# Tokens in their own order in x; the values of mixer A and of B's first group made token by token

## The chip, the cores and the metric

One Trainium2 chip, one of its cores. The metric is the time of one execution in microseconds of device time. The engines are named as in the profile: PE (matrix products; PEld is its loading of the stationary operand), DVE (vector), ACT (scalar), POOL, and SP, whose queue issues most DMAs.

## The reference, cut to what matters

x has 512 tokens of 1024 channels. One product makes queries, keys and values for two mixers, which read the same tokens:

```
proj = h @ w_in
qa, ka, va, qb, kb, vb = split(proj)                # rotation on the first 16 of every 64 channels of q and k
o_a = windowed attention, 16 query heads on 4 key heads, |i - j| <= 128, with a sink, blocks of 128 queries
o_b = for 4 head slots, three groups with (window, dilation) (128, 1), (512, 4), (2048, 16), merged by denominators
gates = sigmoid(h @ w_gate + b_gate)
mixed = g_a * (o_a @ w_br_a) + g_b * (o_b @ w_br_b)
h = layer_norm(a * h + mixed @ w_out)
h = layer_norm(a * h + (silu(h @ w_ff_gate) * (h @ w_ff_up)) @ w_ff_down)
```

Mixer A and the first group of B work on blocks of neighbouring tokens. The second and third groups of B take every 4th and every 16th token, so they work on residues: all tokens with the same remainder of their number by 4.

## The kernel before, in words

Every product is of 32-bit numbers, split in a rounded part (fp32r, "h") and the rest ("l"); one product of two such matrices takes three matrix instructions (h by h, h by l, l by h). A unit is 128 output channels by all 512 tokens: 8 slices of 128 input channels, 24 instructions of 512 columns. Its weights come as two tiles of 256 KB ("ws"), and each tile is split by a copy that rounds (line 333 on ACT or 335 on DVE) and a subtraction on DVE (354) into two slots of the class "whl"; there are 6 ws and 16 whl slots (65).

**x by residue.** The host lays out x so that the 512 columns are residue 0's 128 tokens, then residue 1's, and so on. The start (421 to 432) loads 8 tiles of x, and for each a copy writes the h part (429) and a DVE subtraction the l part (430, 431). With them, slice by slice, run three first units (939 to 942): keys ("k"), queries ("q") and values ("v") of mixer A, with weights cut in pieces of 128, 128 and 256 columns so that the first pieces come early (366 to 386, order by FIRST).

**Queries and keys.** A unit's result goes from PSUM to SBUF; its 32 rotated rows are sent by small DMAs on SP into a common tile (485), rotated by four DVE operations (496 to 502, a "turn", T in the order), and sent back (506). Then q_post (518), k_post (535) and k_sides (553) write the split parts. q_post and k_post bring the columns from residue order into blocks of 128 tokens for mixer A, by runs of 32 floats (510 to 516); k_sides serves the second and third groups, which need residue order, and reads straight on.

**Values** must have the tokens on the partitions. Mixer A's and those of B's first group are made as units, channels on the partitions, then copied (594 to 602) and turned on PE by 128x128 transposes (611), four for each pair of blocks; value_split (617) splits the turned block. The first group's blocks are shifted by 64 tokens. The values of the second and third groups are made directly (632 to 658): x's columns of one residue are the stationary operand, 512 channels of both groups the moving one, 96 instructions (650 to 652).

**Attention.** For mixer A (unit_a, 712) there are 16 blocks: scores (578, 579), a DVE operation that adds the mask (726), exp on ACT (730), a factor (666, 668), transposes of the probabilities (678), products with the values (743, 744), and an addition of two halves that writes the result by residue (754). Mixer B (unit_b, 773) does the same for three groups.

**The order** is not the code's. ORDER (74) names the steps; every operation gets a priority from the work on PE before it, and a scheduler (171) with modelled costs writes each engine's queue once, while the program is built. In ORDER, VA and V0 are the turned values, V the direct ones, q1 to q7 and Q../K.. units, A0 to A3 and B0 to B3 the attention, G and g gates (924), which fill PE; G sends its result to DRAM and it is fetched later. An engine does its queue in order.

Of the kernel before, what the change touches and what calls it, by code (L numbers as in the profile page):

```python
# [15 lines left out]
P = 128  # L16
# [45 lines left out]
FIRST = {("k", 0): (-1000, -998.2, -997.2), ("q", 0): (-998.8, -998.1, -997.1), ("v", 0): (-998.7, -998, -997),  # L62
         ("k", 1): (-996.9,), ("q", 1): (-996.7,), ("v", 1): (-996.6,),
# [11 lines left out]
VA q1 T G q2 A0 q3 q4 G k1 T G A1 q5 G q6 q7 T A2 G G A3 G  # L75
Q00 K00 T V Q02 K02 T V0 Q01 K01 T B0 B1 g Q10 K10 T g Q12 K12 T Q11 K11 T B2 B3 g7
# [212 lines left out]
def hybrid_layer(ctx: ExitStack, tc: tile.TileContext, wpack, xT, xtok, sink, bgate,  # L289
# [40 lines left out]

    def copy(eng, dst, src):
        if eng == ACT:
            nc.scalar.activation(dst, src, AF.Copy)  # L333
        else:
            nc.vector.tensor_copy(dst, src)
# [86 lines left out]
    for j in range(2):  # L422
        for w, u in (("k", U_KA), ("q", U_QA), ("v", U_VA)):
            first[w, j] = half_unit_by(u, j, ((0, S),) if j else CUTS, FIRST[w, j])
    for j in range(KD):
        st, ap = slot(F32, "xs"), FIRST["x"][j]
        load(st, xT[j], abs_prio=ap)
        th, tl = xtok_of(j)
        op(cp_alts(S), lambda e, j=j, st=st: copy(e, xh[j](), st.t), reads=[st], writes=[th], abs_prio=ap)
        op([(DVE, dve(S))], lambda e, j=j, st=st: nc.vector.tensor_tensor(  # L430
            xl[j](), st.t, f32(xh[j]()), op=ALU.subtract), reads=[st, th], writes=[tl], abs_prio=ap)
    cosT, sinT, mA, mB = slot(), slot(), slot(), slot()
    for t_, src, ap in ((cosT, ropec, -119.5), (sinT, ropes, -119.4)):
        for i in range(8):
            op([(POOL, 1.0)], lambda e, t_=t_, i=i, src=src: nc.gpsimd.dma_start(t_.t[16 * i:16 * i + 16], src[0:16]),
               writes=[(t_, i)], abs_prio=ap, moves=0.1)
    load(mA, maska, abs_prio=-119.3, dst=lambda: mA.t[:, :384])
# [36 lines left out]
    class Turn:  # L474
# [16 lines left out]
        def turn(self):  # L491
# [7 lines left out]
               reads=[*toks, *[(cosT, i) for i in range(8)]], writes=[t], prio=EV)  # L499
            op([(DVE, dve(S))], lambda e: nc.vector.tensor_tensor(w.t[r], w.t[r], sinT.t[r], op=ALU.mult),  # L500
               reads=[w, *[(sinT, i) for i in range(8)]], writes=[w], prio=EV)
# [8 lines left out]
    def view(ap, nt, src):  # L510

        if nt == 0:
            return ap
# [21 lines left out]
    def k_post(R, heads, nt):  # L535
# [15 lines left out]
    k_post.head = lambda h, hh, nt: h  # L551
# [32 lines left out]
    def turned_values(u, nt, turn_by=0, done=None):  # L584

        src = []
        w = S // nt
        for i in range(2):
            ps = done
            if i or not done:  # L590
                ps = bank("dense")
                feat_x(ps, unit(u + i))
            t = slot()

            def evac(e, t=t, ps=ps):
                s = view(ps.t, nt, True)
                if turn_by:
                    copy(e, view(t.t[:, turn_by * w:], nt - turn_by, False), s[:, :nt - turn_by])
                    copy(e, view(t.t[:, :turn_by * w], turn_by, False), s[:, nt - turn_by:])
                else:  # L600
                    copy(e, view(t.t, nt, False), s)

            op(cp_alts(S, True), evac, reads=[ps], writes=[t], prio=EV)
            src.append(t)
        res = []
        for b in range(NR):
            pb = bank("tb")

            def turn(e, pb=pb, b=b):
                for i in range(2):  # L610
                    nc.tensor.transpose(pb.t[:, i * P:(i + 1) * P], src[i].t[:, b * P:(b + 1) * P], ident.t)

            op([(PE, 0.22)], turn, reads=[*src, ident], writes=[pb])
            res.append(value_split(pb))
        return res

    def value_split(pb, c0=0):

        t = slot(F32R)
        v = lambda: t.t.rearrange("p (h c) -> p h c", h=4)  # L620
        s = lambda: pb.t[:, c0:c0 + 256].rearrange("p (h c) -> p h c", h=4)
        op(cp_alts(256, True), lambda e: copy(e, v()[:, :, 0:64], s()), reads=[pb],
           writes=[(t, "h"), (t, "room")], prio=EV)
        op([(DVE, dve(256))], lambda e: nc.vector.tensor_tensor(
            v()[:, :, 64:128], s(), f32(v()[:, :, 0:64]), op=ALU.subtract),
           reads=[pb, (t, "h")], writes=[(t, "l")], prio=EV)
        return t

    def vtok(t):
        return [(t, "h"), (t, "l")]  # L630

    def token_values():

        parts_ = []
        for k in range(KD):
            st, h, l = slot(F32, "ws"), slot(F32R, "whl"), slot(F32R, "whl")
            u, c = U_VB + k // 4, (k % 4) * 256
            load(st, wpack[u:u + 3:2, :, c:c + 256].rearrange("g p c -> p g c"),
                 dst=lambda st=st: st.t.rearrange("p (g c) -> p g c", g=2), prio=-LOOK)
            split(st, h, l, prio=-LOOK, hold=[(l, "room")])  # L640
            parts_.append((h, l))
        res = ([], [])
# [957 lines left out]
```

## Time and profile before

| | us |
|---|---|
| median of 3 runs (lowest to highest) | 781.55 (781.13 to 781.97) |
| the profiled execution, its time | 781.53 |
| the profiled execution, its span | 779.8 |
| PE busy in the span | 769.9 |
| DVE busy | 652.5 |
| ACT busy | 480.9 |
| POOL busy | 131.5 |

The span is from the first to the last instruction; the rest of the execution's time lies around it. Busy times of PE overlap from one matrix instruction to the next, so what PE does is read from the starts in the timeline. In a row of the timeline the numbers are start and duration in us, xN says how many instructions were merged, and brackets hold the idle time before it and who ended it. In a group's row stand the busy us, the mean ns of one, and the idle time before them. A window's row has the length, then busy us and count for PE, PEld, DVE, ACT and POOL, then the granted clock of PE (1.00 is full), the DMA share and GB/s.

### The profile page before, as it was taken

Reading aid. Unit: us, or ns where it says so; the run is one execution under the profiler, and the core shown is the slowest. Engines: PE = TensorE matmul, PEld = TensorE weight load, DVE = VectorE, ACT = ScalarE, POOL = GpSimd, SP = SyncE. Lnnn points to the kernel's source line nnn. Section 1 sums busy time; section 2 is a strip of 40 time slices with the busy share of each in tenths; the row PEclk is TensorE's granted clock in tenths of the full one; section 3 lists DMA queues with packets and bytes.
Section 4 is the critical chain, followed back from the end, with each engine's and each line's share of the span. In section 5 each row is a group of like instructions: output and inputs, shape, how many; then the busy total and the mean of one; then the engine's idle time right before and its main releaser. Section 6 shows DMA issues by size and latency. Waiting matters only on the chain.

```text
span 779.8 us, 13408 instructions
## 1 busy us (share of the span) xinstructions
PE 769.9 (99%) x4486; PEld 676.6 (87%) x4486; DVE 652.5 (84%) x1377; ACT 480.9 (62%) x1061; POOL 131.5 (17%) x304
## 2 busy tenths in 40 slices
PE   9999999999999999999999999999999999999996
PEld 5888888888888888888888899999999999999985
DVE  5689889898778999797687999887988889888697
ACT  5557787868757668794341667566655566555631
POOL 4100001100000801600011010242102331123002
PEclk9999999999999999999999999999999999999999
DMA  8642323213132324436373388689867987689102
GB/s 268 217 138 71 99 88 105 83 44 108 57 96 88 104 87 145 142 111 201 121 217 67 109 231 225 155 183 213 227 179 161 241 179 208 182 213 210 52 1 108
DMA packets 64901, 111.79 MB, mean 143 GB/s; under 512 B 8640, under 2 KB 12352, under 8 KB 64832
## 3 DMA queue, kind: packets, MB, share of 16 engines
q1 hardware_dynamic: 52656, 89.37, 35.5%
q0 software_dynamic: 12032, 21.50, 16.5%
q8 instruction: 35, 0.57, 0.3%
q14 instruction: 34, 0.28, 0.1%
q10 hardware_dynamic: 144, 0.07, 0.0%
HBM read 104.09 MB, written 3.93 MB: 139 GB/s over the span
## 4 chain that ended last, share of the span: by engine, by line
PE 93%; DVE 2%; ACT 1%; DMA 1%; issue 1%; SPq 1%; DVEq 0%
PE ps L457 11%; PE ps L456 11%; PE ps L458 11%; PE ps L1314 9%; PE ps L1313 9%; PE ps L1312 9%; PE ps L1441 4%; PE ps L1442 4%; PE ps L1443 4%; PE ps L1077 3%; PE ps L1079 3%; PE ps L1078 3%; PE ps L678 2%; PE ps L579 1%; PE ps L578 1%; PE ps L743 1%
## 5 line engine op out<-in xcount | busy, mean ns | idle before, releaser
L333 ACT ACTIVATE sl<-sl 128x512 fp32r<-128x512 f32 (+5 forms) x446 | 242.5, 571 | 65.9 <-DMA sl<-wpack 16.6
L1196 DVE TENSOR_TENSOR sl<-sl,sl 128x512 fp32r<-128x512 f32 (+3 forms) x304 | 169.9, 604 | 12.1 <-ACT sl L333 7.6
L333 ACT ACTIVATE sl<-ps 128x256 f32<-128x256 f32 (+4 forms) x206 | 88.6, 451 | 114.5 <-PE ps L1314 66.6
L456 PE MATMUL ps<-x,sl 128*128 128x512 f32 x336 | 133.7, 398 | 0.4 <-ACT sl L333 0.3
L457 PE MATMUL ps<-x,sl 128*128 128x512 f32 x336 | 131.9, 393 | 0.2 <-DVE x L430 0.2
L458 PE MATMUL ps<-x,sl 128*128 128x512 f32 x336 | 131.6, 392 | 0.0
L354 DVE TENSOR_TENSOR sl<-sl,sl 128x512 fp32r<-128x512 f32 x130 | 87.0, 687 | 9.3 <-ACT sl L333 6.5
L1266 POOL DMA_DIRECT2D sl<-wpack x44 | 39.8, 970 | 260.1 <-DMA sl<-wpack 111.6
L458 PEld LDWEIGHTS ps<-x,sl 128*128 128x128 f32 x336 | 63.1, 188 | 14.4 <-DVE sl L382 0.7
L1312 PE MATMUL ps<-x,sl 128*128 128x256 f32 x264 | 74.8, 283 | 0.0
L1314 PE MATMUL ps<-x,sl 128*128 128x256 f32 x264 | 74.7, 283 | 0.0
L1313 PE MATMUL ps<-x,sl 128*128 128x256 f32 x264 | 74.7, 283 | 0.0
L456 PEld LDWEIGHTS ps<-x,sl 128*128 128x128 f32 x336 | 63.2, 188 | 12.2 <-ACT x L333 1.0
L457 PEld LDWEIGHTS ps<-x,sl 128*128 128x128 f32 x336 | 63.3, 188 | 12.0 <-DVE x L430 1.8
L1196 DVE TENSOR_TENSOR sl<-sl,ps 128x512 f32<-128x512 f32 (+1 forms) x78 | 47.4, 611 | 25.7 <-PE ps L1314 16.6
L1312 PEld LDWEIGHTS ps<-x,sl 128*128 128x128 f32 x264 | 50.6, 192 | 0.5
L1313 PEld LDWEIGHTS ps<-x,sl 128*128 128x128 f32 x264 | 50.6, 192 | 0.5
L1314 PEld LDWEIGHTS ps<-x,sl 128*128 128x128 f32 x264 | 50.6, 192 | 0.0
L1314 PE MATMUL ps<-tw,sl 128*128 128x256 f32 x176 | 49.8, 283 | 0.0
L1313 PE MATMUL ps<-tw,sl 128*128 128x256 f32 x176 | 49.8, 283 | 0.0
L1314 PE MATMUL ps<-sl,sl 128*128 128x256 f32 x176 | 49.8, 283 | 0.0
L1313 PE MATMUL ps<-sl,sl 128*128 128x256 f32 x176 | 49.8, 283 | 0.0
(149 smaller groups left out, 1808.7 us busy)
## 6 DMA issues: line engine op xcount, KB each, us to landing
sl<-wpack SPq DMA_DIRECT2D x243, 256.0 KB, 3.4
sl<-wpack POOLq DMA_DIRECT2D x44, 256.0 KB, 5.2
wf<-wpack SPq DMA_DIRECT2D x36, 256.0 KB, 4.2
wf<-wpack POOLq DMA_DIRECT2D x36, 256.0 KB, 6.5
sl<-sl SPq DMA_DIRECT2D x88, 32.0 KB, 1.9
sl<-xT SPq DMA_DIRECT2D x8, 256.0 KB, 5.8
sl<-xtok SPq DMA_DIRECT2D x8, 256.0 KB, 2.7
gz<-sl SPq DMA_DIRECT2D x7, 256.0 KB, 2.2
```

The lines of the kernel that those rows point to most:

```text
L333: nc.scalar.activation(dst, src, AF.Copy)
L354: op([(DVE, dve(S))], lambda e: nc.vector.tensor_tensor(l.t, src.t, f32(h.t), op=ALU.subtract), reads=[src, h], writes=[l], prio=prio, abs ...
L456: mm(o, a, x0, start=(k == 0), stop=False)
L457: mm(o, a, x1, start=False, stop=False)
L458: mm(o, b, x0, start=False, stop=(k == nk - 1))
L1196: op([(DVE, dve(w))], lambda e: nc.vector.tensor_tensor(dst(), x(), y(), op=o), reads=reads, writes=writes, prio=prio)
L1266: return op([(POOL, 1.0)], lambda e: nc.gpsimd.dma_start(dst.t, wpack[u, :, j * S:(j + 1) * S], accum_op=ALU.add), reads=[dst], writes=[ds ...
L1312: mm(o, wh, bh[k](), start=(first and k == 0), stop=False, skip_group_check=True)
L1313: mm(o, wh, bl[k](), start=False, stop=False, skip_group_check=True)
L1314: mm(o, wl, bh[k](), start=False, stop=(k == 3), skip_group_check=True)
L1441: mm(ps.t, x0, w[0].t, start=(first and m == 0), stop=False, skip_group_check=True)
L1442: mm(ps.t, x0, w[1].t, start=False, stop=False, skip_group_check=True)
```

## The change

x is written token by token. The data come from DRAM by residue as before; the copies that split x, the rotation tables and the masks put them in order on the way, so that they write every fourth float (by_res and res_by are the two views). The values of A and of B's first group are made like those of the other groups, in one product of 512 columns (256 of A, 256 of B's first group) with 128 neighbouring tokens as the stationary operand, 96 instructions; turned_values and its 16 transposes go. The first group's shift by 64 tokens is made by splitting halves of 64 rows. In the direct values of the second and third groups the stationary operand is now every fourth column of x. Gates are written by residue from PSUM, and the views in q_post, k_sides and the addition of A now read every fourth float where they must go by residue; mixer A's queries and all k_post keys are read straight on.

In the start a second unit of queries ("r") takes the place of the first unit of values; the first tile of x is rounded on DVE alone.

```diff
-VA q1 T G q2 A0 q3 q4 G k1 T G A1 q5 G q6 q7 T A2 G G A3 G
-Q00 K00 T V Q02 K02 T V0 Q01 K01 T B0 B1 g Q10 K10 T g Q12 K12 T Q11 K11 T B2 B3 g7
+q2 VA T G A0 q3 q4 G k1 T A1 q5 G q6 q7 T A2 G G A3 G Q00 K00 T V Q02 K02 T Q01 K01 T B0 B1 g Q10 K10 T g Q12 K12 T Q11 K11 T B2 B3 g8
...
+    def by_res(ap):
+        return ap.rearrange("p (i r) -> p r i", r=4)
+    def res_by(ap):
+        return ap.rearrange("p (r i) -> p r i", r=4)
...
-        op(cp_alts(S), lambda e, j=j, st=st: copy(e, xh[j](), st.t), reads=[st], writes=[th], abs_prio=ap)
+        op(cp_alts(S)[1 if j == 0 else 0:], lambda e, j=j, st=st: copy(e, by_res(xh[j]()), res_by(st.t)), reads=[st], writes=[th], abs_prio=ap)
         op([(DVE, dve(S))], lambda e, j=j, st=st: nc.vector.tensor_tensor(
-            xl[j](), st.t, f32(xh[j]()), op=ALU.subtract), reads=[st, th], writes=[tl], abs_prio=ap)
+            by_res(xl[j]()), res_by(st.t), by_res(f32(xh[j]())), op=ALU.subtract), reads=[st, th], writes=[tl], abs_prio=ap)
...
+        op(cp_alts(S), lambda e, t_=t_, raw=raw: copy(e, by_res(t_.t), res_by(raw.t)), reads=[(raw, i) for i in range(8)],
+           writes=[t_], abs_prio=ap + 1)
...
-        if nt == 0:
+        if nt is None:
             return ap
-        if src:
-            return ap.rearrange("p (r t i) -> p t r i", r=4, t=nt)
-        return ap.rearrange("p (t r i) -> p t r i", r=4, t=nt)
+        if nt == 0:
+            return by_res(ap) if src else res_by(ap)
+        return ap.rearrange("p (t i r) -> p t r i" if src else "p (t r i) -> p t r i", r=4, t=nt)
...
-                src = lambda i=i, a=a: R.t[a:a + 64, 256 * i:256 * i + 256].rearrange("p (r c) -> p r c", r=2)
+                src = lambda i=i, a=a: by_res(R.t[a:a + 64])[:, 2 * i:2 * i + 2]
...
+                for n, u in enumerate((U_VA, U_V0)):
+                    op([(SP, 0.37)], lambda e, st=st, n=n, u=u, k=k: nc.sync.dma_start(
+                        st.t[:, 256 * n:256 * n + 256].rearrange("p (g c) -> p g c", g=2),
+                        wpack[u:u + 2, :, k * P:k * P + P].rearrange("g p c -> p g c")), writes=[(st, n)], prio=-LOOK)
...
-                    a, b = xh[k]()[:, r * P:(r + 1) * P], xl[k]()[:, r * P:(r + 1) * P]
+                    c = slice(r, S, 4) if dilated else slice(r * P, (r + 1) * P)
+                    a, b = xh[k]()[:, c], xl[k]()[:, c]
...
+                value_split(ps, 256, (low, (res[1][r], high)), (high, (res[1][(r + 1) % NR], low)))
...
-                x, y = [v[0:64].rearrange("p (m a r i) -> p m a r i", m=2, a=2, r=4)[:, :, a] for v in (o.t, t.t)]
+                x, y = [v[0:64].rearrange("p (m a i r) -> p m a r i", m=2, a=2, r=4)[:, :, a] for v in (o.t, t.t)]
...
-        op([(ACT, act(S, True, 1))], lambda e: nc.scalar.activation(t.t, ps.t, AF.Identity, bias=bg.t[:, f:f + 1]),
+        op([(ACT, act(S, True, 1))], lambda e: nc.scalar.activation(
+            res_by(t.t), by_res(ps.t), AF.Identity, bias=bg.t[:, f:f + 1]),
```

The queues change with it. DVE's at the start, before and then after; sl_76 is the first tile of x as it came, sl_71 and sl_78 are weight pieces of k and q:

```order
L335 CAST sl_131<-sl_78 128x128
L382 TENSOR_TENSOR sl_126<-sl_71,sl_125 128x128
L382 TENSOR_TENSOR sl_132<-sl_78,sl_131 128x128
L430 TENSOR_TENSOR x_141<-sl_76,x_128 128x512
L382 TENSOR_TENSOR sl_139<-sl_80,sl_138 128x128
```

```order
L342 CAST x_131<-sl_76 128x4x128
L389 TENSOR_TENSOR sl_129<-sl_71,sl_128 128x128
L437 TENSOR_TENSOR x_143<-sl_76,x_131 128x4x128
L389 TENSOR_TENSOR sl_135<-sl_78,sl_134 128x128
L389 TENSOR_TENSOR sl_140<-sl_80,sl_139 128x128
```

The rounding of x's first tile, on ACT before, heads DVE's queue, and the rest of that tile comes one operation earlier.

PE's queue where mixer A's values are made, before (in the unit of q1, ps_375) and after (behind the unit of q2, ps_345); sl_329 and sl_382 hold values with channels on the partitions:

```order
L458 MATMUL ps_375<-x_128,sl_284 128x512
L611 MATMUL ps_388<-ident,sl_329 128x128
L611 MATMUL ps_388<-ident,sl_382 128x128
L611 MATMUL ps_391<-ident,sl_329 128x128
L611 MATMUL ps_391<-ident,sl_382 128x128
L456 MATMUL ps_375<-x_128,sl_283 128x512
```

```order
L486 MATMUL ps_345<-x_210,sl_294 128x512
L661 MATMUL ps_402<-sl_301,x_131 128x512
L662 MATMUL ps_402<-sl_302,x_131 128x512
L663 MATMUL ps_402<-sl_301,x_143 128x512
L661 MATMUL ps_402<-sl_313,x_131 128x512
L662 MATMUL ps_402<-sl_314,x_131 128x512
```

The transposes stood between other products; now 96 products with x as the stationary operand stand in one block, each with a weight tile of its own kind (sl_301 and sl_302 are h and l of the first). PE's queue is 16 instructions shorter.

ACT's queue behind the last tile of x, before and after; sl_267 and sl_284 are the rounded weights of the next unit, sl_263 and sl_270 the two masks, sl_290 a rotation table:

```order
L333 ACTIVATE x_203<-sl_111 128x512
L333 ACTIVATE sl_267<-sl_182 128x512
L333 ACTIVATE sl_274<-sl_190 128x512
L333 ACTIVATE sl_283<-sl_192 128x512
L333 ACTIVATE sl_292<-sl_217 128x512
```

```order
L340 ACTIVATE x_210<-sl_111 128x4x128
L340 ACTIVATE sl_263<-sl_113 128x4x32 x2
L340 ACTIVATE sl_270<-sl_118 128x4x16 x4
L340 ACTIVATE sl_270<-sl_118 128x256
L340 ACTIVATE sl_284<-sl_188 128x512
L340 ACTIVATE sl_290<-sl_74 128x4x128
L340 ACTIVATE sl_293<-sl_193 128x512
```

Seven copies of masks have come in ahead of the next unit's weights, and one of a rotation table between them.

More of the change, by code (lines that the diff above doesn't have):

```diff
@@ L581, in scores @@
         return go, [(qt, "h"), (qt, "l"), (kt, "h"), (kt, "d"), (kl, "h"), (kl, "d")]
[L584 to L627, printed above, removed]
+    def value_split(ps, c0, *rows):
+        v = lambda t, d: t.t[d].rearrange("p (h c) -> p h c", h=4)
+        for r, (t, d) in rows:
+            src = lambda r=r: ps.t[r, c0:c0 + 256].rearrange("p (h c) -> p h c", h=4)
+            op(cp_alts(256, True), lambda e, src=src, t=t, d=d: copy(e, v(t, d)[:, :, 0:64], src()), reads=[ps],
+               writes=[(t, "h", d.start), (t, "room", d.start)], prio=EV)
+            op([(DVE, dve(256))], lambda e, src=src, t=t, d=d: nc.vector.tensor_tensor(
+                v(t, d)[:, :, 64:128], src(), f32(v(t, d)[:, :, 0:64]), op=ALU.subtract),
+               reads=[ps, (t, "h", d.start)], writes=[(t, "l", d.start)], prio=EV)
@@ L629, in vtok, with token_values @@
     def vtok(t):
-        return [(t, "h"), (t, "l")]
-    def token_values():
+        return [(t, w, d) for w in "hl" for d in halves[t]]
+    halves = {}
+    def token_values(dilated):
         parts_ = []
@@ L636, in token_values @@
             st, h, l = slot(F32, "ws"), slot(F32R, "whl"), slot(F32R, "whl")
[L637 to L640, printed above, removed]
-            parts_.append((h, l))
-        res = ([], [])
+            if dilated:
+                u, c = U_VB + k // 4, (k % 4) * 256
+                load(st, wpack[u:u + 3:2, :, c:c + 256].rearrange("g p c -> p g c"),
+                     dst=lambda st=st: st.t.rearrange("p (g c) -> p g c", g=2), prio=-LOOK)
+                toks = [st]
+            else:
+                for n, u in enumerate((U_VA, U_V0)):
+                    op([(SP, 0.37)], lambda e, st=st, n=n, u=u, k=k: nc.sync.dma_start(
+                        st.t[:, 256 * n:256 * n + 256].rearrange("p (g c) -> p g c", g=2),
+                        wpack[u:u + 2, :, k * P:k * P + P].rearrange("g p c -> p g c")), writes=[(st, n)], prio=-LOOK)
+                toks = [(st, 0), (st, 1)]
+            op(cp_alts(S), lambda e, h=h, st=st: copy(e, h.t, st.t), reads=toks, writes=[h, (l, "room")], prio=-LOOK)
+            op([(DVE, dve(S))], lambda e, h=h, l=l, st=st: nc.vector.tensor_tensor(
+                l.t, st.t, f32(h.t), op=ALU.subtract), reads=[*toks, h], writes=[l], prio=-LOOK)
+            parts_.append((h, l))
+        res = [[slot(F32R) for _ in range(NR)] for _ in range(2)]
+        every, low, high = slice(0, P), slice(0, 64), slice(64, P)
+        for g in range(2):
+            for t in res[g]:
+                halves[t] = (0, 64) if g and not dilated else (0,)
         for r in range(NR):
```

72 lines of the change are left out of this document (44 added, 28 removed).

## The prediction

> **What bounds the kernel now.** I read the page's totals, the chain that ended last, PE's waits, then the windows and timelines of the stretches that the change touches. The page first:
>
> ```profile
> span 779.8 us, 13408 instructions
> PE 769.9 (99%) x4486; PEld 676.6 (87%) x4486; DVE 652.5 (84%) x1377; ACT 480.9 (62%) x1061; POOL 131.5 (17%) x304
> ...
> PE 93%; DVE 2%; ACT 1%; DMA 1%; issue 1%; SPq 1%; DVEq 0%
> ```
>
> A busy PE need not be PE at its peak, so PE's waits come next (who, for whom, us, times, longest):
>
> ```profile
> PE ps L409 <- DVE eps L443: 1.2, 1, 1.2
> PE ps L456 <- ACT sl L333: 0.3, 1, 0.3
> PE ps L457 <- DVE x L430: 0.2, 1, 0.2
> ```
>
> PE waits 1.7 us in all, at the start. What is left is its own pace, from PE's timeline (start, duration), around the first transposes and in the channel mixer:
>
> ```profile
> 29.07 0.39 PE L456 MATMUL ps<-x,sl 128*128 128x512 f32 x1
> ...
> 30.20 0.39 PE L458 MATMUL ps<-x,sl 128*128 128x512 f32 x1
> 30.43 0.60 PE L611 MATMUL ps<-ident,sl 128*128 128x128 f32 x4
> 30.79 0.48 PE L456 MATMUL ps<-x,sl 128*128 128x512 f32 x1
> 31.10 0.40 PE L457 MATMUL ps<-x,sl 128*128 128x512 f32 x1
> ...
> 560.47 0.28 PE L1312 MATMUL ps<-sl,sl 128*128 128x256 f32 x1
> 560.59 0.28 PE L1313 MATMUL ps<-sl,sl 128*128 128x256 f32 x1
> ```
>
> From 29.07 to 30.20 are five steps: a 512-column product starts every 0.227 us; a 256-column one every 0.12. The time is PE's queue laid end to end. Only three things can move it: fewer or slower PE instructions, a later start, or an engine that falls behind PE.
>
> The third isn't far away. Windows (length, then PE, PEld, DVE, ACT, POOL busy) and two steps of the chain:
>
> ```profile
> 40.00:220.00 180.00, 180.00 (x917) 152.94 (x916) 154.15 (x371) 132.02 (x304) 12.46 (x60) 1.00 0.27 86
> 260.00:280.00 20.00, 20.00 (x102) 16.89 (x101) 18.27 (x45) 11.94 (x26) 11.60 (x37) 1.00 0.31 95
> 280.00:300.00 20.00, 19.89 (x111) 16.88 (x110) 18.43 (x47) 15.61 (x37) 0.27 (x2) 1.00 0.28 85
> ...
> 289.38 0.28 DVE sl L668
> 289.70 0.77 PE ps L678 x5
> ```
>
> In mixer B's stretch (260 to 300) DVE is idle 1.73 and 1.57 us in 20, and the chain goes through DVE up to 289.7. In mixer A's (40 to 220) it is idle 25.8 of 180.
>
> **The change, part by part.** The span is 779.8 us in an execution of 781.53, against a median of 781.55 (781.13 to 781.97), so 1.7 lie outside it and the profiled execution stands for the median.
>
> *PE instructions.* Before, the values of A and of B's first group take 2 x 48 products of 512 columns and 16 transposes. After, 96 products of 512 columns and none. Only the transposes go:
>
> ```profile
> L611 PE MATMUL ps<-ident,sl 128*128 128x128 f32 x16 | 2.4, 272 | 0.0
> ```
>
> From 30.20 to 31.10 are 0.90 us for what would be two steps, 0.454: four transposes cost 0.45, with the delay that they leave to the next product. Four such groups: **-1.8 us**. There is little else to gain: PE has no other waits.
>
> *Strided data.* Tokens now lie in order, and everything that wants them by residue (token mod 4) reads or writes every fourth float, 16 bytes apart. No row of before shows such an operand; the smallest runs in it are 32 floats. The only two rates that one shape shows on DVE are these:
>
> ```profile
> L335 DVE CAST sl<-sl 128x512 fp32r<-128x512 f32 x16 | 6.7, 425 | 0.1
> L335 DVE CAST sl<-ps 128x512 fp32r<-128x512 f32 x6 | 4.0, 686 | 1.4 <-PE ps L678 1.3
> L528 DVE TENSOR_TENSOR sl<-sl,sl 64x512 fp32r<-64x512 f32 x28 | 19.3, 688 | 1.0
> L563 DVE TENSOR_TENSOR sl<-sl,sl 64x256 fp32r<-64x256 f32 x16 | 6.5, 418 | 0.4
> L754 DVE TENSOR_TENSOR tw<-ps,sl 64x256 f32<-64x256 f32 x32 | 13.3, 416 | 2.0 <-ACT sl L333 1.5
> ```
>
> 686/425 is 1.6. I bound a strided operand between 1 (free) and 1.6 squared, 2.6, and take 1.6, one such step: +0.41 on 688 ns, +0.25 on 418. [...]
>
> *The start.* PE, DVE and ACT there:
>
> ```profile
> 4.87 0.50 PE L456 MATMUL ps<-x,sl 128*128 128x512 f32 x1
> 5.59 0.50 PE L457 MATMUL ps<-x,sl 128*128 128x512 f32 x1 [0.22 <-DVE x L430]
> ...
> 10.11 0.49 PE L456 MATMUL ps<-x,sl 128*128 128x512 f32 x1 [0.31 <-ACT sl L333]
> ...
> 12.81 0.43 PE L457 MATMUL ps<-x,sl 128*128 128x512 f32 x1
> ...
> 23.40 0.39 PE L458 MATMUL ps<-x,sl 128*128 128x512 f32 x1
> ...
> 4.15 0.28 DVE L335 CAST sl<-sl 128x128 fp32r<-128x128 f32 x1 [3.00 <-DMA sl<-wpack]
> ...
> 4.85 0.69 DVE L430 TENSOR_TENSOR x<-sl,x 128x512 fp32r<-128x512 f32 x1
> ...
> 12.00 0.69 DVE L430 TENSOR_TENSOR x<-sl,x 128x512 fp32r<-128x512 f32 x1 [0.51 <-ACT x L333]
> ...
> 11.33 0.63 ACT L333 ACTIVATE x<-sl 128x512 fp32r<-128x512 f32 x1 [0.62 <-DMA sl<-xT]
> ...
> 19.68 0.63 ACT L333 ACTIVATE sl<-sl 128x512 fp32r<-128x512 f32 x1 [1.57 <-DMA sl<-wpack]
> ```
>
> Each tile of x is rounded (ACT) and its rest formed (DVE) into a strided tile. The fourth shows the chain without slack: landing at 11.33, ACT 0.63, DVE 12.00 to 12.69, PE at 12.81. At 1.6 times ACT adds 0.38 and DVE 0.41: the product starts 0.8 later, and since the tiles come one by one from the DMA, this is paid once and not eight times. The first tile's rounding moves from ACT to the head of DVE's queue, where a weight piece was rounded: at best 0.43, at 1.6 times 1.1 us from about 4.15, then 0.2 for a weight piece's rest and 0.7 to 1.1 for the tile's, so that is there at 5.5 to 6.6 instead of 5.54 (4.85 + 0.69); the 0.3 us wait at 10.11 takes up part, and the fourth tile's 0.8 the rest. **+0.8 us**, between 0 and 1.6 (twice as dear).
>
> Also here, on ACT between the last tile and the next weights (19.68): seven of the eight small mask copies (the other is DVE's), and the two tables' copies spread over the weights. ACT waits 1.57 us there for DMA; the first weights, used by PE after 23.4 + 0.2, would be late only if they were ready (19.68 + 0.63 + 0.69) 2.6 us later. The mask's four loads stand in SP's queue where one stood, and the rotation tables' loads stay on POOL. Zero, between 0 and 1: what ACT would then add if the cover were gone. The values' weights come as 16 DMAs of 128 KB for 8 tiles, ahead of other weights on SP. Of 16 weight slots the first units hold 12 and the next q unit 4, so the last tile's split (0.63 + 0.69 us) follows that unit's end, 21 products (4.8 us) before its use: covered. The splits by halves of 64 rows add four small operations on each of ACT and DVE, 0.4 us each, where the turned values' copies went: zero.
>
> *The order.* One more q unit and both values come before the first turn, so the turn's DMAs have 120 products of cover instead of some 60; one gate fewer goes to DRAM and back, on SP: zero both, since PE waits for neither now.
>
> *Mixer A.* The 32 additions of L754 read every fourth float: 32 x 0.25 = 8 us on DVE against its 25.8 idle: covered, zero; at 2.6 times 21 us, still inside it. The gates' evacuation on ACT reads PSUM by residue: ACT is idle 48 of 180 there; zero.
>
> *Mixer B.* A rotation turn of one Q and one K unit (second and third groups) has two 64x512 subtractions and four 64x256 ones: 2 x 0.41 + 4 x 0.25 = 1.8 us more on DVE. With one turn in 20 us against 1.73 and 1.57 idle, 0.1 and 0.2 are short, and there are two such pairs of turns: 0.6. The two turns with the first group's Q have 0.8 us more each, outside these windows. **+0.6 us**, between 0 (the idle time covers it) and 7.2 (four turns, nothing covered).
>
> *The dilated values.* Their stationary operand is now every fourth column of x, 96 loads:
>
> ```profile
> L650 PEld LDWEIGHTS ps<-sl,x 128*128 128x128 f32 x32 | 6.0, 188 | 0.9
> L1312 PEld LDWEIGHTS ps<-x,sl 128*128 128x128 f32 x264 | 50.6, 192 | 0.5
> ```
>
> With 256 columns each load fits a step of 0.12 us in spite of its 192 ns, so it holds its path for 0.12 at most. At 1.6 times that is 0.19, under the 0.227 of a 512-column step: zero. At 2.6 it is 0.31, and 96 x 0.09 = 8.3 us come out: the upper bound. [...]
>
> Sum: 781.53 - 1.8 + 0.8 + 0.6 = **781.1 us**: no difference. About 0.2% (1.6 us) is what a measurement of this kernel tells from no change.
>
> **The rivals.** *Strides are free, or all under cover* (a chance of 0.24): only the transposes count, 781.53 - 1.8 = 779.7, faster. For it: 128 us of idle DVE. Against: the tight chain at 11.33 to 12.81.
>
> *DVE falls behind in mixer B* (0.19), slower. It decides where a turn's extra work exceeds the 1.65 us idle in 20. At twice the time (+0.69 and +0.42) a turn adds 3.1, 1.4 short, 5.6 in four turns; the start pays 1.3: 781.53 - 1.8 + 1.3 + 5.6 = 786.6 with nothing made up, 783.1 to 786.6 with some. [...] For it: DVE's 18.3 and 18.4 of 20, and the chain at 289.7. Against: the first group's values leave this stretch, with some 2 us of DVE work (four subtractions of 0.42 and a copy), and B as a whole has idle time on both sides.
>
> *The strided weight load comes out from under its product* (0.12), slower: it decides above 1.9 times (0.227/0.12). At 2.6: 781.1 + 8.3 = 789.4. For it: loads alone, 188 ns, aren't far below 227. Against: only one step of 1.6 is seen anywhere.
>
> **How the numbers follow.** My forecast (the strides eat the gain) has 0.45, with a range of its own of 780.0 to 783.1. That gives faster 0.24, same 0.45, slower 0.31. 779.5 to 786.0 leaves out about 0.05 below (a start that gets earlier) and 0.12 above (most of the third rival, the far end of the second).
>
> **What would show it.** Right: no L611 group; 96 products of the new values at 0.227 us; x's subtractions at 1.1 us and ACT's x copies at 1.0; the 72nd product of the start 0.8 us later (23.4 before); turns' 64x512 subtractions at 1.1; PE's waits in mixer B under a microsecond. Wrong: strided rows at 0.69 (then the first rival), PE waits of several us behind DVE after a turn (the second), dilated products more than 0.23 apart (the third), or weights that come late to the first token product, which I put at zero.

## The result and the profile after

The kernel after takes 794.39 us (median of 6 runs, 793.48 to 795.01), against 781.45 for the kernel before (781.06 to 781.97): a ratio of 1.0165, 95% interval 1.0152 to 1.0178. It is slower by 12.9 us; I had forecast 781.1 and a range to 786.0. Three of the six executions take 793.5 to 793.8 at a granted clock of 0.997, three 794.9 to 795.0 at 0.995; the profiled one, with a span of 793.2, is of the second kind.

From the page after: the span, the busy times, and the chain that ended last by engine.

```profile
span 793.2 us, 13417 instructions
PE 774.7 (98%) x4470; PEld 681.6 (86%) x4470; DVE 671.9 (85%) x1379; ACT 496.9 (63%) x1071; POOL 133.1 (17%) x304
...
PE 79%; DVE 7%; ACT 4%; DMA 2%; issue 2%; SPq 0%; DVEq 0%; ACTq 0%
```

PE still looks busy, but the chain runs over it for 79% of the span and no longer for 93%; 7% go to DVE and 4% to ACT. DVE has 19.4 us more work than before, ACT 16.0. PE's waits (for whom, us, times, longest) were three rows and 1.7 us before:

```profile
PE ps L693 <- ACT sl L681: 2.4, 4, 1.1
PE ps L484 <- ACT sl L340: 1.9, 1, 1.9
PE ps L485 <- DVE x L437: 1.7, 3, 0.6
PE ps L818 <- ACT sl L340: 1.2, 1, 1.2
PE ps L416 <- DVE eps L471: 1.2, 1, 1.2
PE ps L486 <- DVE sl L361: 1.0, 1, 1.0
PE ps L885 <- DVE sl L717: 0.8, 1, 0.8
```

These come to 10.2 us, 5.5 behind ACT and 4.7 behind DVE. The rest doesn't show as a wait. Windows of 20 us (length; PE, PEld, DVE, ACT and POOL busy; granted clock):

```profile
40.00:60.00 20.00, 17.09 (x68) 13.42 (x67) 17.09 (x33) 12.49 (x24) 2.32 (x11) 0.91 0.42 133
...
280.00:300.00 20.00, 19.37 (x97) 15.32 (x96) 18.56 (x41) 15.08 (x29) 1.03 (x7) 1.00 0.33 105
```

So there are two places. One is at 40 to 60, with the granted clock at 0.91 besides; the other is mixer B. Take all pairs of neighbouring product starts, and sum by how much each distance exceeds its columns at 0.227 us for 512. From 40 to 60 this sum is 0.2 us before and 5.0 after; from 160 to 360 it is 10.9 before and 21.5 after; from 60 to 160, mixer A, 7.4 before and 6.1 after.

The first place on PE's timeline, where the block of token products ends and the next unit, a gate, begins:

```profile
51.32 0.39 PE L663 MATMUL ps<-sl,x 128*128 128x512 f32 x1
53.60 0.50 PE L484 MATMUL ps<-x,sl 128*128 128x512 f32 x1 [1.89 <-ACT sl L340]
53.93 0.40 PE L485 MATMUL ps<-x,sl 128*128 128x512 f32 x1
55.35 0.80 PE L486 MATMUL ps<-x,sl 128*128 128x512 f32 x1 [1.02 <-DVE sl L361]
55.94 0.63 PE L484 MATMUL ps<-x,sl 128*128 128x512 f32 x1
...
58.50 0.44 PE L484 MATMUL ps<-x,sl 128*128 128x512 f32 x1
```

From 51.32 to 58.50 are ten steps, 2.27 us at full pace; they took 7.18. PE waits 1.89 for a rounded weight tile and 1.02 for its rest, and after that six steps from 55.94 to 58.50 are 0.427 apart: the granted clock is 0.66 from 55 to 60 and 0.50 from 56 to 58, in all 3.4 us at half speed. The six steps lose 1.2 us. What ACT did meanwhile:

```profile
44.49 1.95 ACT L340 ACTIVATE sl<-sl 64x512 fp32r<-64x512 f32 x3 [2.27 <-DMA sl<-sl]
46.68 0.63 ACT L340 ACTIVATE sl<-sl 64x512 fp32r<-64x512 f32 x1 [0.24 <-DMA sl<-sl]
47.32 1.17 ACT L340 ACTIVATE sl<-ps 128x256 fp32r<-128x256 f32 x3
48.51 3.25 ACT L340 ACTIVATE sl<-sl 64x512 fp32r<-64x512 f32 x5
52.52 0.38 ACT L340 ACTIVATE sl<-ps 64x256 fp32r<-64x256 f32 x1 [0.75 <-DVE sl L342]
52.91 3.75 ACT L340 ACTIVATE sl<-sl 128x512 fp32r<-128x512 f32 x7
```

The block's 16 slots are all read until its last quarter, from about 46 on. The first copy of a new weight into them is at 52.91, behind nine copies of the turn's posts (64x512; the posts are q_post, k_post and k_sides, which follow a turn) and the splits of the values, in order. Six of the nine start after 46. For 0.75 us before the last split ACT itself waits for a DVE copy, which stands behind three of the posts' subtractions on DVE.

The strided operations themselves, from the groups (busy us, mean ns of one):

```profile
L437 DVE TENSOR_TENSOR x<-sl,x 128x512 fp32r<-128x512 f32 x8 | 8.6, 1104 | 2.3 <-ACT x L340 2.2
L340 ACT ACTIVATE x<-sl 128x512 fp32r<-128x512 f32 x7 | 7.5, 1133 | 2.8 <-DMA sl<-xT 2.7
L340 ACT ACTIVATE sl<-sl 64x512 fp32r<-64x512 f32 x46 | 34.0, 739 | 12.3 <-DMA sl<-sl 10.5 <-DVE sl L572 0.6 <-ACT sl L340 0.2
L556 DVE TENSOR_TENSOR sl<-sl,sl 64x512 fp32r<-64x512 f32 x28 | 23.8, 850 | 1.4 <-ACT sl L340 0.4
L340 ACT ACTIVATE sl<-sl 64x256 fp32r<-64x256 f32 x39 | 21.8, 570 | 1.1 <-DVE sl L591 0.4
L769 DVE TENSOR_TENSOR tw<-ps,sl 64x256 f32<-64x256 f32 x32 | 19.3, 602 | 3.1 <-ACT sl L340 2.8
L942 ACT ACTIVATE sl<-ps,bg 128x512 f32<-128x512 f32 x16 | 10.8, 682 | 0.7 <-PE ps L486 0.6
L591 DVE TENSOR_TENSOR sl<-sl,sl 64x256 fp32r<-64x256 f32 x16 | 9.6, 606 | 0.4
```

x's subtraction went from 688 to 1104, 1.6 times, the factor that I took; the 64x256 ones from 418 to 606, 1.45 times. The mean 850 of L556 mixes 16 straight and 12 strided ones, and the two L340 rows of 64 partitions are mixed likewise.

### The profile page after: what moved, and what is told of

It is laid out like the page before. It is cut to its first block, busy times and chain, and to the rows that moved or that the text cites. A ratio compares the mean times of both kernels' runs of the same rounds, so it can differ in the third digit from the quotient of the medians.

```text
span 793.2 us, 13417 instructions
## 1 busy us (share of the span) xinstructions
PE 774.7 (98%) x4470; PEld 681.6 (86%) x4470; DVE 671.9 (85%) x1379; ACT 496.9 (63%) x1071; POOL 133.1 (17%) x304
## 4 chain that ended last, share of the span: by engine, by line
PE 79%; DVE 7%; ACT 4%; DMA 2%; issue 2%; SPq 0%; DVEq 0%; ACTq 0%
PE ps L1328 9%; PE ps L1327 9%; PE ps L1326 9%; PE ps L486 7%; PE ps L484 7%; PE ps L485 7%; PE ps L1455 4%; PE ps L1456 4%; PE ps L1457 4%; ACT sl L340 3%; PE ps L1091 3%; PE ps L1092 3%; PE ps L1093 3%; PE ps L693 2%; DMA sl<-sl 2%
## 5 line engine op out<-in xcount | busy, mean ns | idle before, releaser
L340 ACT ACTIVATE sl<-sl 128x512 fp32r<-128x512 f32 (+5 forms) x460 | 258.9, 594 | 70.9 <-PE ps L485 20.0
L340 ACT ACTIVATE sl<-ps 128x256 f32<-128x256 f32 (+4 forms) x199 | 85.4, 446 | 114.7 <-PE ps L1328 66.5
L484 PE MATMUL ps<-x,sl 128*128 128x512 f32 x304 | 121.3, 399 | 2.0 <-ACT sl L340 1.9
L485 PE MATMUL ps<-x,sl 128*128 128x512 f32 x304 | 119.8, 394 | 1.7 <-DVE x L437 1.7
L486 PE MATMUL ps<-x,sl 128*128 128x512 f32 x304 | 119.9, 394 | 1.0 <-DVE sl L361 1.0
L361 DVE TENSOR_TENSOR sl<-sl,sl 128x512 fp32r<-128x512 f32 x114 | 75.9, 685 | 8.8 <-ACT sl L340 7.9
L486 PEld LDWEIGHTS ps<-x,sl 128*128 128x128 f32 x304 | 57.5, 189 | 14.1 <-DVE sl L361 1.5
L484 PEld LDWEIGHTS ps<-x,sl 128*128 128x128 f32 x304 | 57.6, 190 | 12.7 <-ACT sl L340 3.2
L485 PEld LDWEIGHTS ps<-x,sl 128*128 128x128 f32 x304 | 57.6, 189 | 12.6 <-DVE x L437 3.3
L1327 PEld LDWEIGHTS ps<-x,sl 128*128 128x128 f32 x264 | 50.6, 192 | 0.5
L1326 PEld LDWEIGHTS ps<-x,sl 128*128 128x128 f32 x264 | 50.6, 192 | 0.5
L1328 PEld LDWEIGHTS ps<-x,sl 128*128 128x128 f32 x264 | 50.6, 192 | 0.0
L1328 PE MATMUL ps<-tw,sl 128*128 128x256 f32 x176 | 49.8, 283 | 0.0
L1327 PE MATMUL ps<-tw,sl 128*128 128x256 f32 x176 | 49.8, 283 | 0.0
L1328 PE MATMUL ps<-sl,sl 128*128 128x256 f32 x176 | 49.8, 283 | 0.0
L1326 PE MATMUL ps<-tw,sl 128*128 128x256 f32 x176 | 49.8, 283 | 0.0
```

What stands on the lines that cost most here:

```text
L361: op([(DVE, dve(S))], lambda e: nc.vector.tensor_tensor(l.t, src.t, f32(h.t), op=ALU.subtract), reads=[src, h], writes=[l], prio=prio, abs ...
L484: mm(o, a, x0, start=(k == 0), stop=False)
L485: mm(o, a, x1, start=False, stop=False)
L486: mm(o, b, x0, start=False, stop=(k == nk - 1))
L1326: mm(o, wh, bh[k](), start=(first and k == 0), stop=False, skip_group_check=True)
L1327: mm(o, wh, bl[k](), start=False, stop=False, skip_group_check=True)
```

## The experiments

Theory 1: the order. The block holds every weight slot and ends while ACT is on the turn's posts, so PE starves. Theory 2: time that strided operands add on ACT and DVE. Theory 3: the strided stationary loads. Each time stands against runs of the kernel before on the same chip (781.28 to 781.69).

**flat_all: every stride taken out, queues unchanged.**

```diff
     def by_res(ap):
-        return ap.rearrange("p (i r) -> p r i", r=4)
+        return ap.rearrange("p (r i) -> p r i", r=4)
...
-                    c = slice(r, S, 4) if dilated else slice(r * P, (r + 1) * P)
+                    c = slice(r * P, (r + 1) * P)
```

and the like in the copies of x, the views of the posts and the addition of A.

> The changed kernel with every operand straight that is strided by 16 bytes: x's copies and subtractions, tables, masks, gates, the posts of the turns, mixer A's addition, the stationary loads of the dilated values. The queues stay word for word; the numbers land in other columns, so attention works on other tokens. Theory 1 (the order costs it: the block of 96 token products holds all 16 weight slots, and PE then starves): the stall at 51 to 58 us stays, 786 to 788. Theory 2 (strided operands cost all of it): 780 to 781, no stall. Theory 3 (strided stationary loads): included here, same as theory 2.

785.80 (ratio 1.0059, 1.0044 to 1.0074). 8.6 us of the 12.9 are strides, to about 1 us, and the stall isn't. PE in flat_all at the same place:

```profile
50.75 0.39 PE L663 MATMUL ps<-sl,x 128*128 128x512 f32 x1
53.64 0.50 PE L484 MATMUL ps<-x,sl 128*128 128x512 f32 x1 [2.50 <-ACT sl L340]
```

The block ends 0.57 earlier than in after, and PE goes on at the same time (53.64 and 53.60): the moment isn't set by the block's end.

**turn_first: only the order changed.**

```diff
-q2 VA T G A0 q3 q4 G k1 ...
+T q2 G VA A0 q3 q4 G k1 ...
```

> The changed kernel with another order in its first stretch: the turn before the unit of q2, then q2 and one gate, then the block of token products (T q2 G VA A0 ... instead of q2 VA T G A0 ...). All strides stay. Theory 1 (ACT is still on the turn's posts when the block ends, so the next weights are rounded late and PE stops): the posts are done before the block ends, the stall at 51 to 58 us goes, 789.4. Theory 2 (strides): nothing gained, 794.

790.53 (1.0117, 1.0102 to 1.0133): 3.9 less. The rows of ACT in turn_first that answer to those above:

```profile
40.48 4.57 ACT L340 ACTIVATE sl<-sl 64x512 fp32r<-64x512 f32 x7 [3.63 <-DMA sl<-sl]
...
53.00 3.74 ACT L340 ACTIVATE sl<-sl 128x512 fp32r<-128x512 f32 x7
```

The posts end at 45, the seven weight copies start while the block still runs (its last product starts at 56.87), and no step of PE between 40 and 60 is late by more than 0.1 us. So the order makes this stall; what the slots have to do with it shows in whl20 below. The profiled executions differ by 5.2 us, the medians by 3.9; the 1.2 us at half speed are in the profiled one of after, and by their clock, 0.997 against 0.995, and their time, 1.2 us less, three of its six executions lack them. In mixer B turn_first has other waits, the longest of them:

```profile
PE ps L885 <- DVE sl L717: 2.0, 1, 2.0
```

**flat_turn_first: both.**

> Both edits at once: all strides straight (as in flat_all, other tokens) and the turn before the block of token products (as in turn_first). If order and strides are two separate costs that add: 794.4 - 8.6 - 3.9 = 781.9. If with both gone the whole saving of the transposes shows (781.3 - 1.8): 779.5. If something else costs as well (the bigger turn, the 16 loads, the halves): 784 or more.

780.08 (0.9983, 0.9973 to 0.9992), 1.35 below the kernel before. Order and strides make up the whole loss, but they aren't simply added: the order is worth 3.9 with strides and 5.7 without, the strides 8.6 in the old order and 10.5 in the new. Its waits on PE are four, 2.8 us. So most of the transposes' saving is there; 1.8 was forecast.

**flat_posts: which strides.** Only q_post and k_sides read and write straight.

```diff
-            return by_res(ap) if src else res_by(ap)
-        return ap.rearrange("p (t i r) -> p t r i" if src else "p (t r i) -> p t r i", r=4, t=nt)
+            return res_by(ap)
+        return ap.rearrange("p (t r i) -> p t r i", r=4, t=nt)
...
-                src = lambda i=i, a=a: by_res(R.t[a:a + 64])[:, 2 * i:2 * i + 2]
+                src = lambda i=i, a=a: res_by(R.t[a:a + 64])[:, 2 * i:2 * i + 2]
```

> The changed kernel with the posts of the turns straight (q_post and k_sides read and write their columns as they lie, so mixer B's operands hold other tokens); x's copies, the addition of A, tables, gates and loads stay strided, the queues stay. Theory 2, as the traces now divide it (with all strides gone, 9 us of gaps between PE's products vanish from 160 to 360 us): the posts carry most of it, 787.5. If it is the addition of A, the gates or the loads: 793 to 794.

787.30 (1.0076, 1.0060 to 1.0093): 7.1 of the 8.6 are the posts, again to about 1 us. The same groups in flat_posts, with the same counts:

```profile
L340 ACT ACTIVATE sl<-sl 64x512 fp32r<-64x512 f32 x46 | 29.0, 630 | 12.4 <-DMA sl<-sl 10.6 <-DVE sl L572 0.8 <-ACT sl L340 0.2
L556 DVE TENSOR_TENSOR sl<-sl,sl 64x512 fp32r<-64x512 f32 x28 | 19.2, 687 | 1.0
L340 ACT ACTIVATE sl<-sl 64x256 fp32r<-64x256 f32 x39 | 15.9, 415 | 2.2 <-DVE sl L591 1.4
L591 DVE TENSOR_TENSOR sl<-sl,sl 64x256 fp32r<-64x256 f32 x16 | 6.6, 418 | 0.4
```

On ACT the strides cost 5.0 + 5.9 = 10.9 us, on DVE's subtractions 4.6 + 3.0 = 7.6. PE lost 7.1.

**before_posts, before_copies, before_subs: the posts' strides alone, on the queues of before.** before_posts has the strided views in the copies and the subtractions of mixer B's posts (the first group's queries by a like view, left out here), before_copies in the copies only, before_subs in the subtractions only:

```diff
         if nt == 0:
-            return ap
+            return ap.rearrange("p (i r) -> p r i" if src else "p (r i) -> p r i", r=4)
...
-                src = lambda i=i, a=a: R.t[a:a + 64, 256 * i:256 * i + 256].rearrange("p (r c) -> p r c", r=2)
+                src = lambda i=i, a=a: R.t[a:a + 64].rearrange("p (i r) -> p r i", r=4)[:, 2 * i:2 * i + 2]
```

> The kernel before with only the posts of mixer B strided, as after has them (q_post of all three groups and k_sides; its operands then hold other tokens), queues as before. Theory 2 (time on ACT and DVE that no idle time covers): 6 to 7 us more, 787.5 to 788.5. My forecast's size for mixer B (0.6): 782.1. If the posts hurt only together with the new order: under 783.

> The kernel before with only the copies of mixer B's posts strided (28 of 64x512 and 64x256 shape stand mostly on ACT, about 11 us more there in the trace of before_posts); the subtractions read straight, so h and l parts don't match. Queues as before. If the copies on ACT carry the 6.5 us: 786 to 787.5. If DVE's subtractions carry them (my rival): 781.5 to 783. Half and half: 784.5.

> The kernel before with only the subtractions of mixer B's posts strided (7 to 8 us more on DVE in four pairs of turns), the copies straight, so h and l parts don't match. Queues as before. If DVE carries the 6.5 us, as my second rival had it: 785.5 to 787. If the copies on ACT do: 781.5 to 783. By my forecast's own sum (0.1 and 0.2 us short in two pairs of turns): 782.

787.83 (1.0084, 1.0069 to 1.0099), 785.80 (1.0052, 1.0037 to 1.0067) and 785.05 (1.0046, 1.0031 to 1.0061): 6.5, 4.1 and 3.4 more than before. Either part delays PE alone; the sum of the two, 7.5, and the 6.5 of both lie within the intervals of each other. The copies stand mostly on ACT, 10.2 us more there in before_copies and 1.4 on DVE. How it reaches PE shows in the worst stretch. ACT's ten copies of 64x256 in before, then in before_posts:

```profile
282.56 4.54 ACT L333 ACTIVATE sl<-sl 64x256 fp32r<-64x256 f32 x10 [0.90 <-DMA sl<-sl]
```

```profile
285.73 6.22 ACT L333 ACTIVATE sl<-sl 64x256 fp32r<-64x256 f32 x10 [0.77 <-DMA sl<-sl]
...
293.24 0.51 ACT L668 ACTIVATE sl<-sl,st 128x256 f32<-128x256 f32 x1
```

They start 3.2 us later and take 1.7 us longer, and the factor of the probabilities (L668) stands behind them, and three more copies, in ACT's queue. PE in before_posts waits for that:

```profile
291.59 0.27 PE L680 MATMUL ps<-ident,sl 128*128 128x128 f32 x1
293.80 0.44 PE L680 MATMUL ps<-ident,sl 128*128 128x128 f32 x2 [1.94 <-ACT sl L668]
...
295.93 0.63 PE L457 MATMUL ps<-x,sl 128*128 128x512 f32 x1
296.36 0.63 PE L458 MATMUL ps<-x,sl 128*128 128x512 f32 x1
```

ACT was busy 14.3 us in that window of 20, DVE 18.3: an engine that is idle 5.7 us in 20 still set the end here, because the factor stood behind thirteen copies in its queue, from 285.73 to 293.24.

**evac_res: the reordering moved to where it is free.** turn_first, but mixer B's second and third groups are put by residue when a unit is copied out of PSUM; the turn uses the tables as loaded, and the posts read straight.

```diff
-            op(cp_alts(S, True), lambda e: copy(e, raw.t, ps.t), ...
+            op(cp_alts(S, True), lambda e: copy(e, res_by(raw.t), by_res(ps.t)) if res else copy(e, raw.t, ps.t), ...
...
-               t.t[r], t.t[r], cosT.t[r], op=ALU.mult), ...
+               t.t[r], t.t[r], ct.t[r], op=ALU.mult), ...
```

> turn_first with the reordering of mixer B's second and third groups taken out of the posts: the copy from PSUM to SBUF that every unit needs reads PSUM by residue (the gates' evacuation does so at 682 ns, as straight before), the turn uses the tables as they were loaded (by residue), and q_post and k_sides read straight. Same result as the reference. If the posts' strided reads of SBUF are the cost and a strided read of PSUM is free: turn_first less most of the 7.1 that flat_posts gained, 784 to 785. If a strided read costs the same wherever it is: one copy of 512 columns for each unit instead of its posts, 787 to 788. If the queues alone did it: 790.5.

783.58 (1.0032, 1.0019 to 1.0045): 7.0 less than turn_first. The group of these copies on ACT:

```profile
L340 ACT ACTIVATE sl<-ps 128x512 f32<-128x512 f32 x14 | 8.2, 587 | 0.1
```

587 ns with strided reads of PSUM among them, 588 before where all were straight; the last two on DVE, strided as well, take 684 and 682, and turn_first's straight ones 684 in the mean. It is the fastest kernel here with the whole of the change in it, and still 2.3 us above the kernel before.

**before_load and flat_load: the stationary loads.** before_load puts the stride into the 96 products of before, flat_load takes it out of after.

```diff
-                    a, b = xh[k]()[:, r * P:(r + 1) * P], xl[k]()[:, r * P:(r + 1) * P]
+                    a, b = xh[k]()[:, r:S:4], xl[k]()[:, r:S:4]
```

> The kernel before with one edit: the stationary operand of its 96 direct products is every fourth column of x, as after has it (here it then takes other tokens). Queues as before. Theory 3 by the upper bound: 8.3 us more, 789.8. By the gaps in the trace of after: 2 more, 783.5. Hidden, as I forecast: 781.5.

> The changed kernel with the stationary operand of the 96 dilated products straight (128 neighbouring columns instead of every fourth), nothing else. Theory 3 (a strided load comes out from under its product): 8 us less by my upper bound, 786; by the gaps that the trace of after shows between those products (about 2 us over 96), 792.3. If the load stays under its product: 794.4, as after.

before_load: 782.91 (1.0020, 1.0010 to 1.0029), 1.6 more. flat_load: 795.18 (1.0174, 1.0159 to 1.0189), no gain. The loads in before_load, and PE around the beginning of a run of them in after:

```profile
L650 PEld LDWEIGHTS ps<-sl,x 128*128 128x128 f32 x32 | 9.9, 310 | 0.1
```

```profile
187.07 0.60 PE L693 MATMUL ps<-ident,sl 128*128 128x128 f32 x4
187.43 0.60 PE L661 MATMUL ps<-sl,x 128*128 128x512 f32 x1
187.86 0.40 PE L662 MATMUL ps<-sl,x 128*128 128x512 f32 x1
188.10 0.40 PE L663 MATMUL ps<-sl,x 128*128 128x512 f32 x1
```

A load is 310 ns instead of 188, 1.65 times. Inside a run of 512-column products it stays nearly hidden (0.24 from one start to the next), but behind short products, here four transposes, the load runs late (the second product's starts at 187.62, 0.19 after the first product, and takes 0.33) and the second product comes 0.43 after the first. In after such places, each up to 0.21 late, make most of 2.0 us of gaps in these products; in flat_load the gaps are 0.5. In the profiled pair PE gains 1.0 us over these products, but flat_load's time doesn't show it, and why stays open in part. What its trace adds is how much the clock can hide. PE in flat_load at the first stall:

```profile
53.74 0.50 PE L484 MATMUL ps<-x,sl 128*128 128x512 f32 x1 [1.76 <-ACT sl L340]
...
55.83 0.39 PE L484 MATMUL ps<-x,sl 128*128 128x512 f32 x1
```

The same two waits, 1.76 and 1.02 us, are followed here by no slow step: from 55.83 on the distance is 0.227 again. Whether the clock falls differs between executions, by 1.2 us or more, as much as the effect that is looked for. Three of flat_load's four executions have a granted clock of 0.993 and 0.994, below all six of after, and take 795.05 to 796.31; the fourth, at 0.997, takes 793.84, no less than after's at 0.997.

**flat_start and turn_first_start: x's copies and subtractions straight**, in the order of after and in that of turn_first (x then lies by residue, so attention takes other tokens).

```diff
-        op(cp_alts(S)[1 if j == 0 else 0:], lambda e, j=j, st=st: copy(e, by_res(xh[j]()), res_by(st.t)), ...
+        op(cp_alts(S)[1 if j == 0 else 0:], lambda e, j=j, st=st: copy(e, res_by(xh[j]()), res_by(st.t)), ...
...
-            by_res(xl[j]()), res_by(st.t), by_res(f32(xh[j]())), op=ALU.subtract)
+            res_by(xl[j]()), res_by(st.t), res_by(f32(xh[j]())), op=ALU.subtract)
```

> The changed kernel with only the copies and subtractions of x straight. By my forecast of the start: 0.8 us less, 793.6. If strided writes of x cost more than that (they also stand ahead of weight pieces): up to 2 less, 792.4. If nothing hangs on them: 794.4.

> turn_first with the copies and subtractions of x straight. The 72nd product of the start comes 0.7 us later in after than in before, yet with x straight and the old order nothing was gained (795.5). If the stall behind the values' block took up that 0.7, it shows here, where the stall is gone: 789.8. If the start's delay is taken up elsewhere in any case: 790.5.

795.47 (795.23 to 795.97; 1.0181, 1.0166 to 1.0197) and 790.29 (788.34 to 791.24; 1.0114, 1.0097 to 1.0131). The 72nd product, the last of the three first units, starts at 23.39 in flat_start, 24.12 in after and 23.40 in before: the delay is 0.72 and comes from these strides. The medians show no clear gain. In the old order the block ends 0.73 earlier and PE goes on 0.49 earlier (53.11), but then twelve steps, up to 60.57, run at half speed where after has six: that takes 1.2 us, and from 61 on PE is later than in after. In the new order, where no step is slow in the profiled executions, PE is 0.8 us ahead of turn_first after the start and 1.4 at the end; the medians differ by 0.24, with runs that spread over 2.9. So whether the end feels the 0.7 stays open.

**whl20: 20 weight slots instead of 16, four fewer for the rest.**

```diff
-N_WS, N_WHL, N_ATT, N_WHL1, N_TWO = 6, 16, 16, 40, 4
+N_WS, N_WHL, N_ATT, N_WHL1, N_TWO = 6, 20, 16, 40, 4
```

> The changed kernel with 20 weight slots for 16 (4 fewer for everything else), all else as it is; the planner writes other queues. If the block of token products starves PE because it holds every slot: the next unit's first half is ready when the block ends, the stall at 51 to 58 us goes, 789.5. If the turn's posts, late and ahead of the weights on ACT, are the cause, more slots alone leave half of it or more: 792 to 794.

804.37 (1.0291, 1.0274 to 1.0309), 10 worse than after and outside what either theory gave. The new queues differ in much, but the stall at the block's end is gone, as theory 1 had it. The first weight tile behind the block's own eight is split on DVE at 35.01, while the block runs; in after its turn comes at 54.62. The block's last product starts at 52.12, and the next unit follows at once:

```profile
35.01 0.69 DVE L361 TENSOR_TENSOR sl<-sl,sl 128x512 fp32r<-128x512 f32 x1 [1.91 <-ACT sl L340]
...
52.34 0.39 PE L484 MATMUL ps<-x,sl 128*128 128x512 f32 x1
...
61.04 0.58 PE L606 MATMUL ps<-sl,sl 128*128 128x256 f32 x1 [3.09 <-DVE sl L556]
```

Now the posts are late instead. Seven of their copies stand on ACT at 57.63, behind seven copies of further weights from 50.65 on; the first scores of mixer A wait 3.09 us for one of their subtractions, and eleven steps at half speed follow. Over the whole profile 26 steps are at half speed, about 5 us. How much of the rest is due to the slots taken from other uses, or to the new queues, the run doesn't tell.

**costs_turn_first: the planner (the scheduler that writes the queues) told what the strided operations take.**

```diff
-            op(cp64(), lambda e, t=t, a=a, hr=hr: copy(
+            op(cp64() if nt is None else [(ACT, 1.15), (DVE, 0.75)], lambda e, t=t, a=a, hr=hr: copy(
...
-        lasts.append(op([(DVE, 0.67)], add, ...
+        lasts.append(op([(DVE, 1.3)], add, ...
```

> turn_first with the planner told the measured costs of the strided posts and of the addition of A (64x512 copies 1.15 on ACT and 0.75 on DVE, subtractions 1.2; 64x256 0.6, 0.4 and 0.65; addition 1.3), so that it writes other queues; the work is the same and the result too. If PE waits because the planner counts on shorter posts: 786 to 788. If the time on ACT and DVE itself is what's missing: 790.5, as turn_first.

795.24 (1.0179, 1.0164 to 1.0194), 4.7 slower than turn_first. Truer costs made a worse order, in the start (the 72nd product at 25.48) and in mixer B, and the time lies outside both expectations. So that the planner's ignorance is the cause isn't borne out, and isn't excluded either: the run shows one other set of queues and no more.

## Why the prediction was wrong

*Transposes, -1.8.* Right in kind: with order and strides mended, 1.35 are left (interval 0.6 to 2.1).

*The start, +0.8.* Right on PE: 0.72, at 1104 and 1133 ns for the strided operations. The end doesn't show it clearly. One number in it was wrong: the first tile's rounding on DVE, 0.43, is 0.7 and not 1.1 at 1.6 times; it took 0.63.

*"The order ... zero both, since PE waits for neither now."* This step failed, 3.9 us (5.7 without the strides). I asked whether the values' own weights come in time, and they did. I didn't ask what stands behind the block. A unit passes its slots on as it goes; 96 products with 16 slots pass none on for three quarters of their 21.8 us, so the next unit's rounding is squeezed into the last quarter. There ACT had six of the turn's nine copies in front, and the splits of the values. turn_first, with the posts done before, and whl20, with four more slots, both have no stall there. The turn itself wasn't late (its first DVE operation at 39.26, before at 38.99); nor did "120 products of cover" for it help, since its cost is not its DMAs but the posts behind them. That PE can go on at half speed behind such waits, for 3.4 us in after's trace and not at all in flat_load's, wasn't in the sum either.

*"Mixer B ... +0.6 us."* This step failed, 7.1 us in after and 6.5 on the queues of before. The prices were near (0.38 us more for a 64x512 subtraction and 0.19 for a 64x256 one, forecast 0.41 and 0.25), and so was DVE's total: 7.2 in four pairs of turns and 1.6 for the first group's queries, 7.6 measured for both. Two errors. I counted only DVE, and the posts' copies, which read the same strided rows, add 10.9 us on ACT; before_copies shows that the copies alone cost 4.1. And I set a turn's extra work against the idle time of a window. But idle time was no cover for a chain in order: copy, subtraction, copy and, behind them on the same queue, the next factor, for which PE waits 1.94 us in before_posts. The second rival, DVE falling behind, had the place and a price of 5.6, the upper end of which I took for unlikely; before_subs gives DVE's part as 3.4.

*"At 1.6 times that is 0.19, under the 0.227 of a 512-column step: zero."* The factor was right (310 ns for 188, 1.65), and inside a run the load is nearly hidden (0.24 a step). The step overlooked where runs begin: 1.6 us in before_load. In the changed kernel the gaps are there, but their removal didn't show in the time. The third rival's 8.3 didn't come.

*Mixer A's additions, zero.* Right: 602 ns for 416, 6 us more on DVE, and from 60 to 160 the gaps on PE didn't grow (7.4 before, 6.1 after). *Gates, zero.* Right: 682 ns with a strided read of PSUM, 683 before: ACT's reads show no penalty.

With 1.35 gained and the terms above, 781.45 - 1.35 + 3.9 + 7.1 + 1.6 + 0.7 = 793.4, against 794.39. This fits in size and proves no more: the 1.6 and the 0.7 were measured in before_load and on PE's start and not in the time of after, the costs overlap, as flat_turn_first shows, and after's own executions lie 1.2 apart, at granted clocks of 0.997 and 0.995.

## What to carry to other kernels

When data change their layout, list every reader on every engine with its count, and follow the queue behind each of them: an operation that grows can delay what stands behind it in order, however idle its engine is on average (ACT was idle 5.7 us in 20 in before_posts, and PE waited 1.94 behind it). When work is merged into one longer block, ask when its buffers are handed on and what the engine that refills them is doing just then. Put a reordering on a copy out of PSUM if there is one, since it was free there (587 ns for 588 on ACT) and the operations that did it in SBUF took 1.45 to 1.8 times as long.

## What the runs showed of the hardware

ACT paid for 16-byte steps in SBUF here as DVE did: 1133 ns for 629 at 128x512 where it writes so, 570 for 414 in the mean of the 64x256 copies, of which 25 of 39 are strided; on DVE 1104 for 688 and 606 for 418. Reading PSUM so, ACT paid nothing (587 for 588 and 682 for 683 ns).

PE ran at half speed behind some waits and not behind others. In after waits of 1.89 and 1.02 us within 4 us, and in before_posts of 1.94 and 0.37, were followed by six steps and by some five at 0.427 us, for 0.227 at full pace (granted clock 0.50 in after from 56 to 58); in turn_first a wait of 2.0 us was not, and neither were the 1.76 and 1.02 of flat_load at the place of after's. The same place of the same queues has 6 slow steps in after's trace, 5 in flat_all's, 12 in flat_start's and none in flat_load's. What decides between the two, no run here shows.
